# Attention: VectorE's other work queued behind the last minimum, and the causal mask added to the kept row F

## The chip, the cores and the metric

The kernel runs on one core of one Trainium2 chip. A core has a matrix engine (TensorE, PE in the profile; its weight loads are shown apart as PEld), VectorE (DVE), ScalarE (ACT), GpSimd (POOL) and SyncE (SP), which issues most DMAs. Each engine takes its instructions in the order of its own queue and waits for others by semaphores. On-chip memory is SBUF, 128 partitions wide, and PSUM, into which PE adds its products. The metric is the device time of one execution, in microseconds (us).

## What is computed

One decoder layer over 1024 tokens of 1024 channels: a normed input, one combined projection, a state-space branch and an attention branch of 16 heads with 64 channels, then gated projections of both and an output projection. The change lies in the attention:

```python
scale = ATT_HEAD_DIM ** -0.5
fcum = jnp.cumsum(log_f, axis=-1)
for blk in range(seqlen // ATT_BLOCK):
    q0, q1 = blk * ATT_BLOCK, (blk + 1) * ATT_BLOCK
    s = jnp.einsum('bhqd,bhkd->bhqk', q[:, :, q0:q1], k[:, :, :q1]).astype(jnp.float32) * scale
    s = s + fcum[:, :, q0:q1, None] - fcum[:, :, None, :q1]
    qpos = q0 + jnp.arange(ATT_BLOCK)
    kpos = jnp.arange(q1)
    s = jnp.where(kpos[None, :] <= qpos[:, None], s, -jnp.inf)
    prob = jax.nn.softmax(s, axis=-1)
    outs.append(jnp.einsum('bhqk,bhkd->bhqd', prob.astype(v.dtype), v[:, :, :q1]))
```

`fcum` at the query's own place falls out of the softmax, so only the row F = `fcum` over the keys is needed. The mask concerns one 128x128 square in each block of 128 queries: the one on the diagonal.

## The kernel before

**Two kinds of work are woven together.** All projections are a `Stream` of steps. One step is 12 matmuls of 128x512 into one PSUM bank (`pb`, `pc` or `pd`); `half()` issues half of one. The weights of a step come from DMA into a `raw` tile, or are sums of two or more of them (`total`, L357, and L373, L381). `split` then makes the tile `wop` of two parts: ScalarE rounds the weights (L351) and VectorE subtracts that from the weights (L352). `prepare` does this three steps ahead of the step that is being started, and `load_more` then loads the next `raw` tiles. The other operand of later steps is split too, by `ops.some()` (L278, L281). A finished bank goes out by `keep` (L404, ScalarE) or `give` (L414 to L418, VectorE). Gate products (L1062), stores from GpSimd's queue (L195, L1063, L1533) and a chain of subtractions on GpSimd (L213, in `differences`) come with the steps as small chores.

**The attention loop** goes over eight head pairs (two heads e = 0, 1 in each, in the lower and the upper 64 partitions). A pair has six visits, one for each of `GROUPS` (L1317): a pair of query blocks and a half h of the 1024 keys. In order these are blocks (7,6) with the upper half, (7,6) lower, (5,4) upper, (5,4) lower, (3,2) lower, (1,0) lower. A visit, in the order in which the program issues it:

1. `scores` for both blocks u = 0, 1. For each: six matmuls into two tiles `s`, one for each head. If the block has its diagonal in this half, four more matmuls of a bfloat16 pair (`eye`, `far`) add 1e30 at the keys that lie ahead of the query. Then for each head VectorE adds F to the scores and takes the minimum of the row in one instruction (L1467; F is the tile `fb`, keys sign-flipped so that the minimum is the softmax's shift), and ScalarE takes the exponential with its sum (L1471).
2. `weighted`: the products of the visit before with V, into `av`; after a second half of keys, `free` (L1419) takes `av` out.
3. What was held over (`release`), the small statistics (`settle`, `scale`), and the stream's halves "ahead".
4. `loads` for later visits, and `turned`: the exponentials are transposed on PE into `pt` (L133), and copied out as `p` by ScalarE (L1502) or VectorE (L1500).
5. `out` (L1425, L1431, L1432), then the halves "behind". In these, `ops.some()` is put into a list (`hold`) and done at the next visit's `release`.

So PE's queue reads scores, products, stream, transposes, stream, scores.

**What sets the order.** A scheduler orders each engine's queue by its own estimate of when an instruction is ready. Three tools bind it: `mm`, `turn` and `pin` keep an instruction behind everything written before it on its engine, so PE's order is as written; `tc.high_priority()` puts a block ahead of other ready work; `tc.issue_after(x)` queues everything in a block that is on x's engine behind x. The minima and exponentials are pinned and of high priority. VectorE work that is not pinned may be placed between them, or ahead of the first.

**Tiles that matter.** `fb` holds F for one half of keys and both heads, copied to all partitions, and is one tile for each half; it is loaded in `load_k`, once for a head pair. `small()` gives one of four tiles (tag `th`) that evicted gate values, fetched blocks, `st` and `rb` share. `wop` has four tiles, `raw` six, the scores' and transposes' banks `s` four.

Of the kernel before, what the change touches and what calls it, by code (L numbers as in the profile page):

```python
# [8 lines left out]
F32 = mybir.dt.float32  # L9
# [7 lines left out]
P = 128  # L17
# [69 lines left out]
def hybrid_layer(ctx: ExitStack, tc, a, out):  # L87
# [368 lines left out]
    class Stream:  # L456
# [6 lines left out]
        def __init__(self, pairs, double, last):  # L463
            self.pairs = pairs
            for n, p in enumerate(pairs):
                p.bank, p.other = (pj, "be"[n % 2]), (pjx, "d") if n < double else (pj, "c")

                p.between = n < double or n >= last

            p, q, r = pairs[0:3]  # L470
            self.steps = [(p, 1), (q, 1), (p, 2), (q, 2)] + [(p, n) for n in (6, 5, 7, 4, 3)]
            self.steps += [(q, 6), (q, 5), (q, 7), (r, 1), (q, 4), (q, 3)]
            for n in range(2, last):
                p, nxt = pairs[n], pairs[n + 1]
# [12 lines left out]
            self.building = []  # L487
            self.chores, self.line = [], []
            self.held = None
            self.count = 0  # L490
# [39 lines left out]
        def half(self):  # L530
            if self.run is None:
                if self.at == len(self.steps):
                    return False
                p, which = self.steps[self.at]
                if which == 7 and p.ops is ops_a and "merged" not in fin:
                    return False
                if p.ops is ops_a and not all(p.ops.ready(OPERAND[which].strip("-"), j) for j in range(KH)):
                    return False
                self.ahead(False)
                for ops in self.building:  # L540
                    ops.some(OPERAND[which])
                self.run = p.do(which)
                next(self.run)
            else:
                for _ in self.run:
                    pass
                self.run = None
                p, which = self.steps[self.at]
                if p in self.following:
                    ops = self.following[p]  # L550
                    if ops not in self.building:
                        self.building.append(ops)
                    ops.open(OPERAND[which])
                self.ahead(True)
                self.at += 1
            for ops in self.building:
                if self.held is None:
                    ops.some()
                else:
                    self.held.append(ops)  # L560
# [16 lines left out]

        def release(self):
            held, self.held = self.held or [], None
            for ops in held:  # L580
                ops.some()

        def do_chores(self):
            while self.chores:
# [710 lines left out]
    with tc.tile_pool(name="att", bufs=1, reuse_waits="tile", side="right") as ap, tc.tile_pool(  # L1295
# [1 line left out]
    ) as pp:  # L1297
        rows = [slice(64 * e, 64 * e + 64) for e in range(2)]

        eye = ap.tile([P, 192], BF16, name="eye")  # L1300
        far = ap.tile([P, 192], BF16, name="far")
        nc.vector.memset(eye, 0.0)
        big, beyond = small("big"), small("beyond")
        nc.vector.memset(big[:, 0:192], -NEG)
        for e in range(2):
            nc.vector.tensor_copy(eye[rows[e], 64:P], ident[rows[e], rows[e]])
            nc.gpsimd.affine_select(
                beyond[:, 192 * e : 192 * e + 192], big[:, 0:192], [[1, 192]], ALU.is_gt, 0.0, base=64 * e - 64,
                channel_multiplier=-1,
            )  # L1310
            nc.vector.tensor_copy(far[rows[e], :], beyond[rows[e], 192 * e : 192 * e + 192])

        corner = [(eye[:, 64:192], far[:, 64:192]), (eye[:, 0:P], far[:, 0:P])]

# [123 lines left out]
        def scores(hp, g, u):  # L1438
# [8 lines left out]
            diagonal = h == i // 4  # L1447
            for m, (x, y) in enumerate(ops):
                for e in range(2):
                    mm(  # L1450
                        s[e][:, 0:w], x[rows[e]], y[rows[e]], start=(m == 0), stop=(m == 2 and not diagonal),
                        skip_group_check=True,
                    )
            if diagonal:
                for n, (x, y) in enumerate(corner):
                    for e in range(2):
                        mm(
                            s[e][:, w - P : w], x[rows[e]], y[rows[e]], start=False, stop=(n == 1),
                            skip_group_check=True,
                        )  # L1460
            hd = heads[hp]
            for e in range(2):
                o = ex[:, e, u, 0:w]
                nm = hd.at(hd.nm, i, h, e)
                with tc.high_priority():
                    pin(
                        nc.vector.tensor_tensor_reduce(  # L1467
                            o, s[e][:, 0:w], fb[hp, h][:, e, 0:w], 1.0, 3.0e38, ALU.add, ALU.min, nm
                        )
                    )  # L1470
                    pin(nc.scalar.activation(o, o, AF.Exp, scale=-1.0, bias=nm, accum_out=hd.at(hd.sm, i, h, e)))  # L1471

        def turned(hp, g, sent):

# [157 lines left out]
        for m in range(6 * NK + 1):  # L1632
# [6 lines left out]
                    scores(hp, g, u)  # L1639
            for one in made:  # L1640
                weighted(*one)
            for hd, which in end(m - 1):
                hd.free(which)
            if m == 6 * NK:
                stream.release()
                heads[NK - 1].out(2)
                break
# [87 lines left out]
```

## Time and profile before

| | |
|---|---|
| timed runs | 1293.11, 1295.9 and 4353.94 us; median 1295.9 |
| profiled execution | 1292.21 us, its span 1290.5 us |
| mean granted clock of PE | 0.997 |
| attention loop, first scores to the last pair's end | 685.9 to 1127.7 us |
| minima (L1467) | 192, of 512, 384, 256 and 128 keys |
| mask matmuls | 256, in 32 of the 48 visits |

A profile shows one execution. Rows of its views read: line, engine, operation, output tile `<-` input tiles, shape, count, then busy microseconds and the mean nanoseconds of one. In a view in order of time each row begins with its start and its length in microseconds, and a bracket at the end tells how long the engine had been idle and who released it. In a view of waits a row names the waiting instruction, what ended the wait, and total, times and longest in microseconds. In a view by stretches each engine has its busy time; the last three columns are PE's granted clock, the share of the DMA engines and GB/s.

### The profile page before, as it was taken

The page shows a single profiled execution, that of the slowest core. Times are in us where ns is not written, and L with a number is a line of the kernel's source. Part 1 is how long each engine was busy: PE and PEld are TensorE (multiplying, and loading weights), DVE is VectorE, ACT ScalarE, POOL GpSimd, SP SyncE. Part 2 cuts the span into 40 slices and gives each one's busy share as a digit, 9 for nine tenths or more (in the row PEclk, how much of TensorE's full clock was granted, in tenths as well). Part 3 has the DMA queues.
Part 4 walks back from the last instruction along what each step waited for, and adds up shares of the span by engine and source line. Part 5 has one row for each costly group of instructions (what it writes and reads, how often), then busy time and mean ns, then how long its engine had stood idle before and what let it go on. Part 6 is the DMA issues. An engine that isn't in the chain of part 4 may idle for free.

```text
span 1290.5 us, 20996 instructions
## 1 busy us (share of the span) xinstructions
PE 1254.5 (97%) x7054; PEld 984.4 (76%) x7054; DVE 1006.0 (78%) x1994; ACT 796.5 (62%) x1738; POOL 259.5 (20%) x250
## 2 busy tenths in 40 slices
PE   5999999999999999999999999999999999899997
PEld 3688888887888888888877777777777776578886
DVE  7988886987788878897777567666898768776975
ACT  7745665566665665666546656666886567743754
POOL 4000440013300330124001121220001102146052
PEclk9999999999999999999999999999999999999999
DMA  8232542645336633654365665667877667656932
GB/s 297 69 115 76 161 146 91 199 143 183 128 119 204 176 130 105 212 172 115 132 211 197 203 217 198 199 221 228 256 268 238 198 213 257 205 188 194 362 113 99
DMA packets 153515, 233.57 MB, mean 181 GB/s; under 512 B 15968, under 2 KB 61504, under 8 KB 153408
## 3 DMA queue, kind: packets, MB, share of 16 engines
q1 hardware_dynamic: 137408, 197.14, 48.0%
q10 hardware_dynamic: 11136, 19.11, 3.9%
q0 software_dynamic: 4864, 15.99, 3.2%
q8 instruction: 55, 0.90, 0.3%
q14 instruction: 52, 0.43, 0.1%
HBM read 162.99 MB, written 72.34 MB: 182 GB/s over the span
## 4 chain that ended last, share of the span: by engine, by line
PE 75%; DVE 9%; DMA 7%; ACT 5%; issue 3%; SPq 1%; POOL 0%; DVEq 0%; ACTq 0%; POOLq 0%
PE pb L130 31%; PE pc L130 18%; PE pd L130 6%; PE pt L133 5%; PE av L130 4%; PE s L130 4%; PE yps L130 2%; DVE wop L352 2%; ACT ex L1471 1%; DMA xt<-in_x 1%; PE st L130 1%; DMA raw<-in_wu 1%; DVE ex L1467 1%; DVE sum L357 1%; ACT wop L351 1%
## 5 line engine op out<-in xcount | busy, mean ns | idle before, releaser
L351 ACT ACTIVATE wop<-sum 128x512 fp32r<-128x512 f32 x180 | 112.5, 626 | 113.4 <-DVE sum L357 53.8
L352 DVE TENSOR_TENSOR wop<-sum,wop 128x512 fp32r<-128x512 f32 x180 | 136.2, 758 | 54.2 <-ACT wop L351 53.3
L1471 ACT ACTIVATE ex<-ex,nm 128x512 f32<-128x512 f32 (+1 forms) x192 | 116.2, 606 | 66.1 <-DVE nm L1467 64.8
L404 ACT ACTIVATE s<-pb 128x512 f32<-128x512 f32 x144 | 85.2, 591 | 103.3 <-PE pb L130 102.7
L130 PE MATMUL pc<-x3h,wop 128*128 128x512 f32 x384 | 131.1, 398 | 1.5 <-DVE th L414 1.1
L130 PE MATMUL pb<-x0h,wop 128*128 128x512 f32 x384 | 131.1, 399 | 0.0
L130 PE MATMUL pc<-x2h,wop 128*128 128x512 f32 x384 | 130.8, 398 | 0.1
L130 PE MATMUL pb<-x6h,wop 128*128 128x512 f32 x384 | 129.5, 395 | 1.3 <-ACT s L404 1.3
L130 PE MATMUL pb<-x5h,wop 128*128 128x512 f32 x384 | 129.9, 396 | 0.8 <-ACT s L404 0.7
L130 PE MATMUL pb<-x4h,wop 128*128 128x512 f32 x384 | 129.0, 395 | 0.0
L352 DVE TENSOR_TENSOR wop<-raw,wop 128x512 fp32r<-128x512 f32 x144 | 102.5, 713 | 32.6 <-ACT wop L351 32.3
L1467 DVE CUSTOM_DVE_ANT_0 ex<-s,fb 128x512 f32<-128x512 f32 (+1 forms) x192 | 97.3, 552 | 20.0 <-PE s L130 20.0
L351 ACT ACTIVATE wop<-raw 128x512 fp32r<-128x512 f32 x144 | 89.7, 624 | 22.7 <-PE pc L130 15.2
L130 PE MATMUL pd<-x1h,wop 128*128 128x512 f32 x288 | 96.3, 394 | 0.0
L130 PEld LDWEIGHTS pc<-x3h,wop 128*128 128x128 f32 x384 | 72.5, 189 | 18.9 <-issue 1.6
L130 PEld LDWEIGHTS pb<-x5h,wop 128*128 128x128 f32 x384 | 72.1, 188 | 18.5 <-ACT s L404 2.1
L130 PEld LDWEIGHTS pb<-x6h,wop 128*128 128x128 f32 x384 | 72.1, 188 | 18.4 <-issue 1.7
L130 PEld LDWEIGHTS pb<-x0h,wop 128*128 128x128 f32 x384 | 72.7, 189 | 17.4 <-issue 2.7
L130 PEld LDWEIGHTS pc<-x2h,wop 128*128 128x128 f32 x384 | 72.1, 188 | 18.0 <-issue 2.8
L130 PEld LDWEIGHTS pb<-x4h,wop 128*128 128x128 f32 x384 | 72.1, 188 | 17.0 <-issue 2.2
L133 PE MATMUL pt<-ident,ex 128*128 128x128 f32 x576 | 74.3, 274 | 5.1 <-ACT ex L1471 4.5
L133 PEld LDWEIGHTS pt<-ident,ex 128*128 128x128 f32 x576 | 65.0, 140 | 15.4 <-ACT ex L1471 9.2
(310 smaller groups left out, 2917.8 us busy)
## 6 DMA issues: line engine op xcount, KB each, us to landing
raw<-in_wu SPq DMA_DIRECT2D x128, 256.0 KB
csb<-cs_dram SPq DMA_DIRECT2D x32, 256.0 KB
fb<-f_dram SPq DMA_DIRECT2D x16, 512.0 KB
rb<-st_dram SPq DMA_DIRECT2D x48, 128.0 KB
wd<-in_wo SPq DMA_DIRECT2D x40, 128.0 KB
xt<-in_x SPq DMA_DIRECT2D x8, 512.0 KB
gs_dram<-th ACTq DMA_DIRECT2D x16, 256.0 KB
qh_dram<-th ACTq DMA_DIRECT2D x16, 256.0 KB
```

Of the source, the lines that this page charges most:

```text
L130: return tc.keep_in_program_order(nc.tensor.matmul(*args, **kw))
L133: return tc.keep_in_program_order(nc.tensor.transpose(out_, in_, idn))
L351: nc.scalar.activation(op[:, 0], src, AF.Copy)
L352: nc.vector.tensor_tensor(op[:, 1], src, op[:, 0], ALU.subtract)
L357: self.adds.tensor_tensor(t, x, y, ALU.add)
L404: nc.scalar.activation(s, ps, AF.Copy)
L1467: nc.vector.tensor_tensor_reduce(o, s[e][:, 0:w], fb[hp, h][:, e, 0:w], 1.0, 3.0e38, ALU.add, ALU.min, nm)
L1471: pin(nc.scalar.activation(o, o, AF.Exp, scale=-1.0, bias=nm, accum_out=hd.at(hd.sm, i, h, e)))
```

## The change

Three things. **The mask:** the matmuls of `eye` and `far` go. A tile `beyond` (128x128, float32) holds 1e30 where a key lies ahead of the query and 0 elsewhere, and a new function `corner(hp, i, engine)` adds it in place to the 128 columns of F that belong to block i, for both heads. A minimum that must see these columns unmasked comes earlier in the loop's order, one that must see them masked comes later. For the first block of a visit GpSimd adds, issued in `loads` of the visit before (blocks 5, 3 and 1, and block 7 of the next pair); for the second block VectorE adds, between the minima of the first block and those of the second.

**The order:** `scores` notes its last minimum as `stream.front`. `prepare`, `ops.some()`, `free` and the deferred subtractions (`first`, `second`, `last` in `outputs`) run inside `stream.behind()`, so that their VectorE instructions are queued behind that minimum.

**The hold:** in the halves "behind", `prepare` too is put into the list, and done at the next visit's `release`, with its `load_more`.

```diff
         def prepare(self, p, which):
-            p.prepare(which)
+            if self.held is not None:
+                self.held.append(lambda: self.prepare(p, which))
+                return
+            with self.behind():
+                p.prepare(which)
             self.load_more()
+
+        def behind(self):
+
+            return nullcontext() if self.front is None else tc.issue_after(self.front)
...
         def release(self):
             held, self.held = self.held or [], None
-            for ops in held:
-                ops.some()
+            for fn in held:
+                with self.behind():
+                    fn()
...
-        eye = ap.tile([P, 192], BF16, name="eye")
-        far = ap.tile([P, 192], BF16, name="far")
...
-        corner = [(eye[:, 64:192], far[:, 64:192]), (eye[:, 0:P], far[:, 0:P])]
+        beyond = ap.tile([P, P], F32, name="beyond")
+        big = small("big")
+        nc.vector.memset(big[:, 0:P], -NEG)
+        nc.gpsimd.affine_select(beyond, big[:, 0:P], [[1, P]], ALU.is_gt, 0.0, base=0, channel_multiplier=-1)
...
+        def corner(hp, i, engine):
+
+            f = fb[hp, i // 4][:, :, i % 4 * P : i % 4 * P + P]
+            pin(engine.tensor_tensor(f, f, beyond.unsqueeze(1).to_broadcast([P, 2, P]), ALU.add))
...
-            if diagonal:
-                for n, (x, y) in enumerate(corner):
-                    for e in range(2):
-                        mm(
-                            s[e][:, w - P : w], x[rows[e]], y[rows[e]], start=False, stop=(n == 1),
-                            skip_group_check=True,
-                        )
             hd = heads[hp]
+            if u and h == i // 4:
+                with tc.high_priority():
+                    corner(hp, i, nc.vector)
             for e in range(2):
                 o = ex[:, e, u, 0:w]
                 nm = hd.at(hd.nm, i, h, e)
                 with tc.high_priority():
-                    pin(
+                    least = pin(
                         nc.vector.tensor_tensor_reduce(
                             o, s[e][:, 0:w], fb[hp, h][:, e, 0:w], 1.0, 3.0e38, ALU.add, ALU.min, nm
                         )
                     )
                     pin(nc.scalar.activation(o, o, AF.Exp, scale=-1.0, bias=nm, accum_out=hd.at(hd.sm, i, h, e)))
+            stream.front = least.ins
...
             hp, g = divmod(m, 6)
             more = hp + 1 < NK
+            if g in (1, 3, 4):
+                corner(hp, {1: 5, 3: 3, 4: 1}[g], nc.gpsimd)
+            if g == 4 and more:
+                corner(hp + 1, 7, nc.gpsimd)
...
         for _ in range(14):
             stream.half()
+        corner(0, 7, nc.gpsimd)
...
-            for hd, which in end(m - 1):
-                hd.free(which)
+            with stream.behind():
+                for hd, which in end(m - 1):
+                    hd.free(which)
...
-            for fn in deferred:
-                fn()
+            with stream.behind():
+                for fn in deferred:
+                    fn()
```

More of the change, by code (lines that the diff above doesn't have):

```diff
@@ L489, in __init__ @@
             self.held = None
+            self.front = None
             self.count = 0
@@ L557, in half @@
                 if self.held is None:
-                    ops.some()
+                    with self.behind():
+                        ops.some()
                 else:
-                    self.held.append(ops)
+                    self.held.append(ops.some)
             for chores in (self.chores, self.line):
@@ L579, in release @@
             held, self.held = self.held or [], None
-            for ops in held:
-                ops.some()
+            for fn in held:
+                with self.behind():
+                    fn()
         def do_chores(self):
@@ L1298, in hybrid_layer @@
         rows = [slice(64 * e, 64 * e + 64) for e in range(2)]
-        eye = ap.tile([P, 192], BF16, name="eye")
-        far = ap.tile([P, 192], BF16, name="far")
-        nc.vector.memset(eye, 0.0)
-        big, beyond = small("big"), small("beyond")
-        nc.vector.memset(big[:, 0:192], -NEG)
-        for e in range(2):
[L1306 to L1309, printed above, removed]
-            )
-            nc.vector.tensor_copy(far[rows[e], :], beyond[rows[e], 192 * e : 192 * e + 192])
-        corner = [(eye[:, 64:192], far[:, 64:192]), (eye[:, 0:P], far[:, 0:P])]
+        beyond = ap.tile([P, P], F32, name="beyond")
+        big = small("big")
+        nc.vector.memset(big[:, 0:P], -NEG)
+        nc.gpsimd.affine_select(beyond, big[:, 0:P], [[1, P]], ALU.is_gt, 0.0, base=0, channel_multiplier=-1)
         GROUPS = [((7, 6), 1), ((7, 6), 0), ((5, 4), 1), ((5, 4), 0), ((3, 2), 0), ((1, 0), 0)]
@@ L1446, in scores @@
             ops = [(t[:, x, isl], keys[:, y, 0:w]) for x, y in ((0, 0), (0, 1), (1, 0))]
-            diagonal = h == i // 4
             for m, (x, y) in enumerate(ops):
@@ L1450, in scores @@
                     mm(
-                        s[e][:, 0:w], x[rows[e]], y[rows[e]], start=(m == 0), stop=(m == 2 and not diagonal),
-                        skip_group_check=True,
-                    )
-            if diagonal:
-                for n, (x, y) in enumerate(corner):
-                    for e in range(2):
-                        mm(
-                            s[e][:, w - P : w], x[rows[e]], y[rows[e]], start=False, stop=(n == 1),
-                            skip_group_check=True,
-                        )
+                        s[e][:, 0:w], x[rows[e]], y[rows[e]], start=(m == 0), stop=(m == 2), skip_group_check=True,
+                    )
             hd = heads[hp]
+            if u and h == i // 4:
+                with tc.high_priority():
+                    corner(hp, i, nc.vector)
             for e in range(2):
@@ L1646, in hybrid_layer @@
                 heads[NK - 1].out(2)
+                stream.front = None
                 break
```

## The prediction

> **What bounds the kernel now.** I read the page first, then the stretches of the attention stage, then one visit of it on each engine, then the waits.
>
> ```profile
> PE 1254.5 (97%) x7054; PEld 984.4 (76%) x7054; DVE 1006.0 (78%) x1994; ACT 796.5 (62%) x1738; POOL 259.5 (20%) x250
> ...
> PE 75%; DVE 9%; DMA 7%; ACT 5%; issue 3%; SPq 1%; POOL 0%; DVEq 0%; ACTq 0%; POOLq 0%
> ```
>
> TensorE (PE) is busy 97% of the span and carries 75% of the chain that ended last. The change touches only the attention loop, so I cut that loop into its eight head pairs of six visits (the matmuls `s<-k,q` mark the visits). These are the fifth pair, the eighth, and the sum over all eight; the columns are busy microseconds in that stretch.
>
> ```profile
> 915.90:966.90 51.00, 50.35 (x356) 37.24 (x355) 46.20 (x122) 43.79 (x107) 2.16 (x4) 1.00 0.84 282
> ...
> 1071.20:1127.70 56.50, 51.14 (x350) 36.24 (x349) 44.87 (x109) 40.20 (x101) 11.13 (x14) 1.00 0.74 246
> sum 441.80, PE 434.94 PEld 326.15 DVE 319.87 ACT 296.74 POOL 59.36; mean PE 54.37 PEld 40.77 DVE 39.98 ACT 37.09 POOL 7.42
> ```
>
> PE is idle for 441.8 − 434.9 = 6.9 us of the loop, 5.4 of them in the last pair. VectorE (DVE) is busy 72% (319.9 of 441.8) but 91% in the fifth pair (46.2 of 51.0); GpSimd (POOL) is busy 13%. So two things can shorten the loop: fewer PE instructions, and the 6.9 us. Nothing else on PE changes, and PE's order is written out by the program.
>
> **The change: the matmuls that go.** Two visits on PE, the first with a diagonal block in each half, the second without one, and then a short diagonal visit:
>
> ```profile
> 800.82 0.99 PE L130 MATMUL s<-k,q 64*128 64x512 f32 x6
> 801.62 0.28 PE L130 MATMUL s<-far,eye 64*128 64x128 bf16 x3
> 801.72 0.42 PE L130 MATMUL s<-k,q 64*128 64x384 f32 x1
> ...
> 802.33 0.32 PE L130 MATMUL s<-far,eye 64*128 64x128 bf16 x4
> 802.58 0.87 PE L130 MATMUL av<-p,v 128*64 128x256 f32 x8
> ...
> 811.02 1.66 PE L130 MATMUL s<-k,q 64*128 64x512 f32 x12
> 812.61 1.62 PE L130 MATMUL av<-p,v 128*64 128x256 f32 x14
> ```
>
> ```profile
> 822.21 0.29 PE L130 MATMUL s<-far,eye 64*128 64x128 bf16 x4
> 822.30 0.53 PE L130 MATMUL s<-k,q 64*128 64x128 f32 x6
> 822.67 0.29 PE L130 MATMUL s<-far,eye 64*128 64x128 bf16 x4
> 822.89 1.30 PE L130 MATMUL av<-p,v 128*64 128x256 f32 x10
> ```
>
> ```profile
> L130 PE MATMUL s<-far,eye 64*128 64x128 bf16 x256 | 18.9, 221 | 0.0
> ```
>
> Matmuls overlap, so I count from start to start. From the first mask matmul to the next other one: 0.10 + 0.25 = 0.35 us in the first visit, 0.09 + 0.22 = 0.31 in the short one. A cross-check: the visit without a diagonal takes 1.59 us for 1024 columns of scores, so 896 columns cost 1.39, and the first visit took 1.76, which is 0.37 more. There are 256 / 8 = 32 such visits: 32 x 0.33 = 10.6 us. The ends are 0 (PE waits elsewhere instead) and 18.9, the group's busy time, in which overlap with neighbours counts twice. I take 10.6, since starts are what moves the next instruction.
>
> **The order of VectorE.** In the first visit of the last pair:
>
> ```profile
> 1072.74 0.29 PE L130 MATMUL s<-far,eye 64*128 64x128 bf16 x4
> ```
>
> ```profile
> 1075.78 0.68 DVE L281 TENSOR_TENSOR x0l<-x0l,x0h 128x512 fp32r<-128x512 f32 x1
> 1076.38 0.68 DVE L1467 CUSTOM_DVE_ANT_0 ex<-s,fb 128x512 f32<-128x512 f32 x1
> ...
> 1077.60 0.68 DVE L281 TENSOR_TENSOR x0l<-x0l,x0h 128x512 fp32r<-128x512 f32 x1
> 1078.20 0.55 DVE L1467 CUSTOM_DVE_ANT_0 ex<-s,fb 128x384 f32<-128x384 f32 x1
> ```
>
> ```profile
> 1077.16 0.72 ACT L1471 ACTIVATE ex<-ex,nm 128x512 f32<-128x512 f32 x1 [4.15 <-DVE nm L1467]
> ```
>
> ```profile
> PEld pt L133 <- ACT ex L1471: 9.2, 18, 1.1
> ```
>
> ```profile
> 1129.81 0.27 PE L133 MATMUL tp<-ident,ns 128*8 128x128 f32 x1 [2.13 <-DVE ns L1376]
> ```
>
> The scores lay ready from about 1073.0 and the first minimum (L1467) came at 1076.38, with another split (L281) between the minima. ScalarE then waited 4.15 us, and behind it the transposes (L133). The change puts splits, weight sums and the products of `free` behind the last minimum, and holds the weight work of a visit's later halves over to the next visit. What it can give back is those 6.9 us and the 2.13 us just behind the loop, 9.0 together; `o<-o,rb`, evictions and gate products are not queued, so part of the delay stays. I take 3.5, the ends are 0 and 9.0.
>
> What is late next is the held work, above all the weight halves:
>
> ```profile
> 835.81 0.68 DVE L352 TENSOR_TENSOR wop<-sum,wop 128x512 fp32r<-128x512 f32 x1
> ```
>
> ```profile
> 849.24 0.39 PE L130 MATMUL pc<-x3h,wop 128*128 128x512 f32 x1
> ```
>
> I paired the 78 weight halves of the loop (L352) in order with the steps that use them. Of those made inside the loop, this one has the shortest time from ready to used: 849.24 − 836.49 = 12.75 us. A hold lasts less than one visit, 51.0 / 6 = 8.5 to 56.5 / 6 = 9.4 us. So I cost it at nothing; without that cover each late half would cost PE up to its 0.68 us. On SyncE's queue the weight loads follow the held sums, by the same part of a visit; their tiles are read several steps later, so again nothing, with one 0.68 us stall for each late tile as the other end.
>
> **The adds on VectorE.** 32 adds over 128x256, ahead of the second block's minima.
>
> ```profile
> L1432 DVE TENSOR_TENSOR zr<-o 128x256 f32<-128x256 f32 x16 | 6.8, 423 | 0.3
> ```
>
> 32 x 0.42 = 13.4 us of VectorE. Beside it runs ScalarE: one exponential takes 0.72 us against 0.68 for a minimum, so after two exponentials the third minimum has some slack, and the scores come 0.1 us earlier. On the path I count 0; uncovered it is 0.42 in each of the 18 waits of the transposes, 7.6 us.
>
> **The adds on GpSimd.** 32 of them, each half the size of the subtraction here, so 0.65 us:
>
> ```profile
> 801.87 1.29 POOL L213 TENSOR_TENSOR x<-x,th 128x512 f32<-128x512 f32 x1
> ```
>
> ```profile
> 802.07 1.65 DVE L352 TENSOR_TENSOR wop<-raw,wop 128x512 fp32r<-128x512 f32 x1 [1.06 <-ACT wop L351]
> ```
>
> ```profile
> 715.50 1.28 POOL L213 TENSOR_TENSOR th<-x,th 128x512 f32<-128x512 f32 x1 [17.20 <-DMA th<-ys_dram]
> ```
>
> ```profile
> 716.11 0.69 DVE L1467 CUSTOM_DVE_ANT_0 ex<-s,fb 128x512 f32<-128x512 f32 x1
> ...
> 717.33 0.69 DVE L1467 CUSTOM_DVE_ANT_0 ex<-s,fb 128x512 f32<-128x512 f32 x1
> ```
>
> While GpSimd subtracted, a VectorE subtraction took 1.65 us in place of 0.68; a minimum beside it took its usual 0.69. Hence each of the 32 adds may hold a VectorE instruction by up to 0.65 us, 20.8 us of VectorE in all, but it falls right behind the last minimum, where the queued work is not urgent. Only the fifth pair lacks room: 46.2 + 4 x 0.42 + 4 x 0.65 = 50.5 us of work in 51.0 − 1.3 = 49.7. I count +1, with ends 0 and 20.8. [...]
>
> The adds that follow groups 3 and 4 wait for the last minimum, and what is behind them on GpSimd waits too. The subtraction at 715.50 would start after 718.02 + 0.65 = 718.7, so 3.2 us later, and with it its small tile comes free, one of four that the evictions of PE's banks share. I count +2 for that, from 0 to 3.2 in each of some four such places, 13.
>
> The sum, against the profiled execution (1292.2 us, 1.7 over its span): 1292.2 − 10.6 − 3.5 + 1 + 2 = 1281.1. The two timed runs near it, 1293.1 and 1295.9 (also the median of the three), lie 2.3 above the profiled one in the mean; so I forecast 1281.1 + 2.3 = 1283.
>
> **Rivals.** *The path moves to the minima.* With two halves of PE work or fewer in a visit of the later pairs, PE has less to do between scores and transposes; there the 10.6 would only lengthen the wait. For it: the 18 waits above; against: in the seven pairs before the last PE idles 6.9 − 5.4 = 1.5 us together. Half the gain stays: 1292.2 − 5.3 + 2 = about 1289, 1291 in a timed run.
>
> *GpSimd's holds land on the path.* All 20.8 in place of 1: 1281.1 + 19.8 = 1300.9, timed 1303. It decides where VectorE's work after a minimum is urgent, as an eviction of a PE bank is. Against it: at 802.07 the held subtraction delayed PE nowhere that the waits show. [...]
>
> *Slower: a mask add stuck in GpSimd's queue.* The next visit's first minimum waits for it.
>
> ```profile
> POOL ya_dram L1533 <- DVE zr L1432: 74.2, 6, 30.1
> ...
> POOL ya_dram L1533 <- DVE zr L1425: 57.3, 5, 16.9
> ```
>
> ```profile
> 946.24 0.69 DVE L1467 CUSTOM_DVE_ANT_0 ex<-s,fb 128x512 f32<-128x512 f32 x1
> ...
> 952.54 0.68 DVE L1467 CUSTOM_DVE_ANT_0 ex<-s,fb 128x512 f32<-128x512 f32 x1
> ```
>
> From a last minimum (ending 946.93) to the next first one there are 5.6 us in the tight fifth pair. It decides once a store ahead of the add waits longer than that after the minimum: the 11 waits, less 5.6 each, are 131.5 − 61.6 = 69.9 us; were half of it on the path, 1281.1 + 35.0 = 1316, and all of it 1351; the middle is 1334, timed 1336. Against it: these waits began with GpSimd idle, and the stores belong to an earlier visit (801.32, just as the next one's scores began).
>
> *Much faster.* The group's whole 18.9 and all 9.0: 1292.2 − 27.9 = 1264, timed 1267.
>
> **How the numbers follow.** Forecast 0.58 (1273 to 1290); path moved 0.12; holds 0.15; stuck add 0.11; much faster 0.04. Within 2% (about what a measurement of this kernel can tell from no change; 1270 to 1321) lie the first three: 0.85; faster 0.04, slower 0.11. The low end, 1273, lies just under the sum with the full 9.0 and without the 3 us of new costs (1292.2 − 10.6 − 9.0 = 1272.6, timed 1275); the high end, 1304, takes in the holds. Left out are the stuck add, the much faster case and the tails, some 0.17.
>
> **What would show it.** No `s<-far,eye` rows; diagonal visits about 0.33 us shorter on PE; no split, sum or weight row between minima but the mask add of about 0.42; PE's idle time in the loop under 6.9; PE's row of waits on the minima empty. I am wrong if minima wait for GpSimd, if matmuls `pb` or `pc` wait for weight halves or evictions, or if the transposes wait more than 9.2 us for the exponentials.

## The result, and the profile after

| | before | changed |
|---|---|---|
| median of 18 runs | 1294.09 us | 1291.15 us |
| ratio, first set | | 0.9981 [0.9971, 0.9991] |
| median, second set | 1293.25 us | 1289.84 us |
| ratio, second set | | 0.9972 [0.9959, 0.9984] |
| profiled execution, span | 1292.21, 1290.5 us | 1290.98, 1289.3 us |

The change gains 2.5 to 3.6 us, where 11.1 were forecast against the profiled execution. That it lies within 2% was right, the size was not. In the first execution of the changed kernel (4334.7 us) PE was busy for 4310.5 us with its 6798 matmuls, against the 1249.3 below; it and the 4353.94 of the kernel before are left out, and the profile below is of the second set.

The busy time of each engine in the changed kernel:

```profile
PE 1249.3 (97%) x6798; PEld 982.4 (76%) x6798; DVE 1025.1 (80%) x2021; ACT 798.8 (62%) x1738; POOL 292.7 (23%) x281
```

The 256 instructions are gone, but PE is busy only 5.2 us less (1254.5 to 1249.3). The short diagonal visit of the third pair, in order of time on PE, shows where they were:

```profile
820.26 0.90 PE L130 MATMUL s<-k,q 64*128 64x256 f32 x12
821.09 1.95 PE L130 MATMUL av<-p,v 128*64 128x256 f32 x16
```

The scores take 0.83 us from start to start, where before 1.14 passed (821.75 to 822.89 there): 0.31 less. So did nearly every steady visit (one that waits for nothing) with a diagonal: in the first four pairs the third, fifth and sixth visit went from 8.14, 10.96 and 7.81 us to 7.81, 10.67 and 7.50.

The loop by stretches, one for each pair; the fifth and the eighth, and the sum (busy us of PE, PEld, DVE, ACT, POOL, with instructions; then granted clock, DMA share, GB/s):

```profile
912.10:966.40 54.30, 51.55 (x326) 37.50 (x325) 48.70 (x124) 43.97 (x107) 6.29 (x8) 0.97 0.79 268
...
1067.60:1131.10 63.50, 54.14 (x318) 38.65 (x317) 50.64 (x119) 41.44 (x104) 14.82 (x17) 0.92 0.66 218
sum 445.00, PE 430.92 PEld 324.40 DVE 339.95 ACT 299.63 POOL 89.92; mean PE 53.87 PEld 40.55 DVE 42.49 ACT 37.45 POOL 11.24
```

From first scores to the end of the last pair's transposes the loop took 443.9 us before and 445.0 now: no gain at all in this execution. The lengths of the pairs, counted from scores to scores (the last one to the transposes behind it), tell where:

| pair | 1 | 2 | 3 | 4 | 5 | 6 | 7 | 8 |
|---|---|---|---|---|---|---|---|---|
| before | 57.2 | 57.7 | 57.7 | 57.4 | 51.0 | 49.7 | 54.6 | 58.6 |
| changed | 57.8 | 56.1 | 56.1 | 56.1 | 54.2 | 47.9 | 53.4 | 63.5 |

Five pairs gain 1.3 to 1.8 us each, 7.6 together. The first, fifth and eighth lose 8.7. The clock column shows one part of that loss: in pairs 5 and 8 PE was granted 0.97 and 0.92 of its clock. These are the stretches themselves, in the changed kernel:

```profile
933.80:937.20 3.40, 3.40 (x17) 1.73 (x14) 3.40 (x13) 3.40 (x13) 0.00 (x0) 0.51 0.66 228
1094.20:1097.60 3.40, 3.36 (x10) 2.61 (x11) 3.27 (x9) 1.90 (x7) 0.00 (x0) 0.50 0.40 132
1121.50:1128.30 6.80, 6.80 (x32) 4.63 (x33) 3.20 (x12) 3.41 (x11) 0.54 (x1) 0.50 0.35 120
```

and the only such stretch near the loop in the kernel before, just behind its end:

```profile
1130.20:1133.60 3.40, 3.40 (x14) 2.02 (x12) 2.15 (x4) 2.49 (x6) 0.00 (x0) 0.50 0.09 31
```

At half the clock I count half of these 13.6 us as lost, 6.8 us: an estimate from the clock column. With it the loop adds up to within a microsecond: −10.6 for the matmuls, as forecast, +5.1 for idle PE (9.0 us before, counted to the same end, 14.1 now), +6.8 for the clock: +1.3, where +1.0 was measured. What follows the loop gained 2.5 us (160.7 to 158.2), 1.7 of them the stretch that lay there before. The timed runs show the loss of clock too, but a smaller one: in the second set the mean clock is 0.9943 over the 12 executions of the changed kernel and 0.9966 over the 23 of the kernel before. The difference, 0.0023 of 1290 us, is about 3 us by the same estimate.

PE's waits in the changed loop (waiting instruction, what ended the wait; total us, times, longest), with VectorE's wait for scores on top:

```profile
DVE ex L1467 <- PE s L130: 37.9, 26, 3.2
...
PEld s L130 <- ACT p L1503: 10.2, 11, 3.9
...
PE s L130 <- ACT p L1503: 6.6, 5, 3.5
PEld pt L133 <- ACT ex L1471: 6.6, 13, 1.5
...
PE pt L133 <- DVE nm L1467: 1.9, 1, 1.9
```

And the two rows of the kernel before to compare with:

```profile
DVE ex L1467 <- PE s L130: 20.0, 16, 2.6
...
PEld s L130 <- ACT p L1502: 3.3, 7, 1.2
```

The minima do come sooner: VectorE now waits for scores more than before (37.9 against 20.0 us), and the transposes' loads wait 6.6 us for exponentials instead of 9.2. But the next scores wait for the copies `p` of the transposes: 10.2 us on the loads, where it was 3.3 before, and 6.6 on the matmuls, where it was 1.2. The wait moved from one side of the transposes to the other.

### The profile page after: what moved, and what is told of

It is laid out like the page before. It is cut to its first block, busy times and chain, and to the rows that moved or that the text cites. A ratio compares the mean times of both kernels' runs of the same rounds, so it can differ in the third digit from the quotient of the medians.

```text
span 4333.0 us, 20609 instructions
## 1 busy us (share of the span) xinstructions
PE 4310.5 (99%) x6798; PEld 2214.8 (51%) x6798; DVE 1025.2 (24%) x2021; ACT 826.2 (19%) x1738; POOL 266.2 (6%) x281
## 4 chain that ended last, share of the span: by engine, by line
PE 99%; DVE 0%; ACT 0%; DMA 0%; issue 0%; DVEq 0%; SPq 0%; ACTq 0%
PE pb L130 44%; PE pc L130 25%; PE pd L130 8%; PE pt L133 6%; PE av L130 5%; PE s L130 4%; PE yps L130 2%; PE st L130 1%; PE tr L133 1%; PE tr L130 1%; PE tr_v L133 1%; PE df L130 0%; PE pv L130 0%; PE pt_f L130 0%; PE pt_cs L130 0%; PE pv_t L133 0%
## 5 line engine op out<-in xcount | busy, mean ns | idle before, releaser
L130 PE MATMUL pc<-x3h,wop 128*128 128x512 f32 x384 | 386.9, 1104 | 0.0
L130 PE MATMUL pb<-x6h,wop 128*128 128x512 f32 x384 | 385.6, 1099 | 0.7 <-ACT s L404 0.7
L130 PE MATMUL pb<-x0h,wop 128*128 128x512 f32 x384 | 385.7, 1099 | 0.0
L130 PE MATMUL pb<-x5h,wop 128*128 128x512 f32 x384 | 383.2, 1096 | 0.7 <-ACT s L404 0.7
L130 PE MATMUL pc<-x2h,wop 128*128 128x512 f32 x384 | 383.1, 1096 | 0.0
L130 PE MATMUL pb<-x4h,wop 128*128 128x512 f32 x384 | 382.7, 1093 | 0.0
L130 PE MATMUL av<-p,v 128*64 128x256 f32 (+1 forms) x640 | 239.8, 993 | 0.0
L130 PE MATMUL pb<-x6l,wop 128*128 128x512 f32 x192 | 210.9, 1098 | 0.0
L130 PE MATMUL pb<-x5l,wop 128*128 128x512 f32 x192 | 210.9, 1098 | 0.0
L130 PE MATMUL pb<-x0l,wop 128*128 128x512 f32 x192 | 210.6, 1097 | 0.0
```

The lines of the kernel that those rows point to most:

```text
L130: return tc.keep_in_program_order(nc.tensor.matmul(*args, **kw))
```

## The experiments

Two questions: does the ordering, or do the adds, eat the gain; and can either be dropped? My theory was that the matmuls are worth what was forecast and that the losses come with the rest; the rivals were that the matmuls were never on the path, and that the queueing helps as forecast while the adds cost much more. Effects below are (ratio − 1) x 1293 us, with the interval worked out likewise.

**The matmuls alone.** The kernel before, with the mask left out:

```diff
-                        s[e][:, 0:w], x[rows[e]], y[rows[e]], start=(m == 0), stop=(m == 2 and not diagonal),
+                        s[e][:, 0:w], x[rows[e]], y[rows[e]], start=(m == 0), stop=(m == 2),
...
-            if diagonal:
+            if False:
```

> The kernel before without its 256 mask matmuls; the causal mask is left out altogether, the rest of the computation is as before. It prices the matmuls alone. The prediction's term: 10.6 us under before. Theory A: under 5 us. Theory C: the mean granted clock falls, as in the changed kernel, and a part of the 10.6 us is missing.

Measured 1285.16 us, 0.9941 [0.9926, 0.9957]: −7.6 us [−9.6, −5.6]. In its profile the loop fell from 443.9 to 434.7, 9.2 us, though PE idled 0.5 more. 9.2 + 0.5 = 9.7 us of PE's instructions, so the 10.6 was nearly right as work, and the timed runs got 7.6 of it. Their mean clock was 0.9955, against 0.9966 in the kernel before; that is 1.4 us of the rest, by the estimate from the clock. (The half-clock stretch that begins in the last 2.2 us of this loop cost little there: PE was busy for 0.10 us of them.)

**The order alone.** Queueing and hold as in the change, the mask by matmuls as before:

```diff
+        def behind(self):
+            return nullcontext() if self.front is None else tc.issue_after(self.front)
...
+            with self.behind():
+                p.prepare(which)
...
             if diagonal:
                 for n, (x, y) in enumerate(corner):
```

> The order and the hold as in the change, the mask still by matmuls as before. If the order costs time: 5 to 10 us over before. If it does what the prediction said: 2 to 9 us under before. If it matters to nothing: within 1 us of before.

Measured 1293.07 us, 1.0000 [0.9988, 1.0013]: 0.0 us [−1.6, +1.7]. Nothing is gained. Its fifth pair takes 54.9 us (51.0 before), so that loss needs no add. The first visit of its last pair, at which the prediction had looked, does fall from 11.5 to 8.5 us.

**The mask alone.** The adds as in the change, but no queueing and no hold:

```diff
         def prepare(self, p, which):
-            if self.held is not None:
-                self.held.append(lambda: self.prepare(p, which))
-                return
-            with self.behind():
-                p.prepare(which)
+            p.prepare(which)
             self.load_more()
...
         def behind(self):
...
-            return nullcontext() if self.front is None else tc.issue_after(self.front)
+            return nullcontext()
```

> The mask added to F as in the change, but nothing queued behind the minimum and nothing held over. If the new order costs time (B, by the order), this gains what the matmuls gave, 8 to 12 us under before. If the adds on VectorE and GpSimd cost it (B, by the adds), or the matmuls were worth little (A), 0 to 4 us under before.

Measured 1305.62 us, 1.0095 [1.0076, 1.0114]: +12.3 us [+9.8, +14.7]. Against the kernel with no mask at all, the 64 adds cost 1305.6 − 1285.2 = 20.4 us. The first visit of its second pair, in order of time, shows how:

```profile
745.58 0.68 DVE L1463 CUSTOM_DVE_ANT_0 ex<-s,fb 128x512 f32<-128x512 f32 x1
...
746.19 1.03 DVE L373 TENSOR_TENSOR sum<-sum,raw 128x512 f32<-128x512 f32 x1
...
747.14 0.68 DVE L1421 TENSOR_TENSOR o<-av,zr 128x512 f32<-128x512 f32 x1
...
747.74 0.41 DVE L1337 TENSOR_TENSOR fb<-fb,beyond 128x256 f32<-128x256 f32 x1
...
748.19 0.56 DVE L1463 CUSTOM_DVE_ANT_0 ex<-s,fb 128x384 f32<-128x384 f32 x1
...
749.78 0.33 PE L133 MATMUL pt<-ident,ex 128*128 128x128 f32 x1 [1.25 <-ACT ex L1467]
...
750.79 0.44 PE L133 MATMUL pt<-ident,ex 128*128 128x128 f32 x2 [0.69 <-ACT ex L1467]
```

The add sits between the second and the third minimum, and a sum and a product have slipped in ahead of it. So the third minimum starts 1.9 us after the second one ended, where the add alone takes 0.41, and the transposes wait 1.25 us, then 0.69 more. Counted over the loop, 60 VectorE instructions of over 0.3 us, besides the adds, stand between the minima of a visit here, 28 in the kernel before and 2 in the changed one. Over the loop the loads of the transposes wait for exponentials (9.2 us in the kernel before):

```profile
PEld pt L133 <- ACT ex L1467: 27.0, 33, 2.7
```

**Which of the adds.** As in the kernel just shown, without queueing and hold, and only VectorE's 32 adds; the half of the mask that GpSimd adds is left out:

```diff
-            if g in (1, 3, 4):
-                corner(hp, {1: 5, 3: 3, 4: 1}[g], nc.gpsimd)
-            if g == 4 and more:
-                corner(hp + 1, 7, nc.gpsimd)
...
-        corner(0, 7, nc.gpsimd)
```

> The mask adds without the new order, and of these only VectorE's 32 between the minima; the blocks that GpSimd would mask (7, 5, 3, 1) stay unmasked, so half of the mask is left out. The mask adds without the order cost 20 us over the kernel without a mask (1305.6 against 1285.2). If VectorE's adds between the minima make it, since other work slips in with them: 1300 or more. If GpSimd's adds make it (its queue, or its hold on VectorE): 1285 to 1290.

Measured 1306.58 us, 1.0111 [1.0091, 1.0130]. VectorE's adds make all of it; GpSimd's add nothing that can be seen.

**The order without adds.** The changed kernel without any add; the mask is left out:

```diff
-            if u and h == i // 4:
-                with tc.high_priority():
-                    corner(hp, i, nc.vector)
```

and the calls on GpSimd as above.

> The changed kernel without any mask add, so the causal mask is left out; the order and the hold stay. It prices the 64 adds under the new order. If the adds cost what the changed kernel lost (Q): 8 to 11 us under before, like the kernel without mask matmuls. If the order costs it (L): 3 to 5 us under before, and the fifth pair stays near 54 us against 51.0.

Measured 1285.53 us, 0.9954 [0.9940, 0.9968]: −5.9 us [−7.8, −4.1]. Against no mask and no order (−7.6) the order seems to cost 1.7 us, though the intervals overlap; it gains nothing here either. Against the change itself (−2.5 and −3.6) the adds cost 2.3 to 3.4 us under the order, not 20.

The fourth visit of its last pair lasts 14.5 us where before it took 10.5. The minima are on time, but on ScalarE two splits stand ahead of the exponentials, and the first of them waits 4.10 us for its load; so the transposes wait. Then ScalarE has a split, an eviction, a weight split and four more splits ahead of the first copy, while PE runs at half clock (1097.2 to 1104.0):

```profile
1098.29 0.61 ACT L280 ACTIVATE x1h<-x1l 128x512 fp32r<-128x512 f32 x1
...
1099.29 0.61 ACT L351 ACTIVATE wop<-sum 128x512 fp32r<-128x512 f32 x1
1099.80 1.13 ACT L280 ACTIVATE x5h<-x5l 128x512 fp32r<-128x512 f32 x2
1100.84 1.13 ACT L280 ACTIVATE x3h<-x3l 128x512 fp32r<-128x512 f32 x2
1101.88 0.57 ACT L1500 ACTIVATE p<-pt 128x512 f32<-128x512 f32 x1
```

**The hold.** The changed kernel, `prepare` no longer held over:

```diff
         def prepare(self, p, which):
-            if self.held is not None:
-                self.held.append(lambda: self.prepare(p, which))
-                return
             with self.behind():
```

> The changed kernel, but the weight work of a visit's later halves is not held over; the queueing behind the minimum stays. If the hold makes the lump (L): the fifth pair falls from 54.2 us to about 51, and the kernel is 2 to 4 us faster than the changed one. If the queueing alone makes it: the fifth pair stays at 54. If the hold is what keeps sums and splits from between the minima: 5 us or more slower, towards the kernel with the mask adds alone (1305.6).

Measured 1289.06 us, 0.9982 [0.9966, 0.9997]: the change without its hold is as fast as with it (0.9972, 0.9981). The place of the loss moved: pairs 1, 5 and 8 take 60.0, 51.6 and 58.9 us. So the loss of the fifth pair comes from the hold: the queueing is still there, and the pair is back near the 51.0 of before. In the four kernels with the order and the hold in every pair it takes 53.4 to 54.9 us.

**All adds on VectorE.**

```diff
-                corner(hp, {1: 5, 3: 3, 4: 1}[g], nc.gpsimd)
+                corner(hp, {1: 5, 3: 3, 4: 1}[g], nc.vector)
...
-                corner(hp + 1, 7, nc.gpsimd)
+                corner(hp + 1, 7, nc.vector)
...
-        corner(0, 7, nc.gpsimd)
+        corner(0, 7, nc.vector)
```

> The changed kernel with all 64 mask adds on VectorE, none on GpSimd. Theory Q (an add stuck in GpSimd's queue, and GpSimd holding VectorE): the third visit of the last pair falls from 11.2 us towards 6.8, the fifth from 13.7 towards 10.5, and the kernel gains 3 to 7 us over the changed one. Theory L (VectorE's queue itself, a lump of queued work ahead of an eviction): 32 more adds of 0.42 us make the fifth and the last pair longer, and the kernel is 0 to 5 us slower than the changed one.

Measured 1291.82 us, 0.9996 [0.9983, 1.0009]. Taking GpSimd out of it gains nothing: pairs 1, 5 and 8 take 60.2, 54.4 and 63.0 us. In the last pair the third visit falls from 11.2 to 6.5 us, but the fifth stays at 13.9 (13.7 in the changed kernel). GpSimd's queue is therefore not the main cause.

**The changed kernel again**, unedited:

> The changed kernel once more, for a profile at PE's full rate. Theory A (the mask's matmuls were worth less than 10.6 us on PE): visits with a diagonal are shorter by clearly less than 0.33 us each and PE's idle time in the loop is about as before, 7 us. Theory B (new waits give it back): those visits are shorter by 0.33 us, and PE's idle time, in the loop or behind it, is 8 to 10 us more than before. Theory C (the granted clock gives it back): PE's matmuls start to start take about 0.5% longer, at a mean granted clock of 0.992 to 0.995 against 0.997. Time 2.5 us under the kernel before.

Measured 1289.84 us, 0.9972 [0.9959, 0.9984]; its profile is the one shown above.

**The change where it pays.** If pairs 2 to 4, 6 and 7 gain and the others lose, the others should keep matmuls. First the fifth and the last pair, with narrower mask matmuls (64 columns, or 64 keys). In these kernels `beyond` is a bfloat16 tile, a second difference, not priced apart.

```diff
+        marks = [(eye[:, 64:P], far, 0), (eye, far[:, 0:64], 64)]
+        added = {0, 1, 2, 3, 5, 6}
...
         def corner(hp, i, engine):
+            if hp not in added:
+                return
...
-            stream.front = least.ins
+            stream.front = least.ins if hp in added else None
```

and `prepare` is held only while `front` is set.

> The change in six head pairs; in the fifth and the last the mask is by matmuls (over 64 columns of queries or keys in place of 128, to fit) and nothing is queued or held. If the loss sits in these two pairs, as the visits say: the fifth near 51, the last near 58.6, the others as in the changed kernel, the loop 437 us against 444.0, and the kernel 6 to 8 us under before. If it is spread, or moves on to the next pair: 2 to 4 us under before.

Measured 1289.67 us, 0.9972 [0.9957, 0.9987], the same as the change, though its profiled loop took 437.8 us.

Then the first pair as well:

```diff
-        added = {0, 1, 2, 3, 5, 6}
+        added = {1, 2, 3, 5, 6}
```

> As the hybrid, and the first head pair too has its mask by matmuls, with nothing queued or held. If the adds cost only in visits where VectorE or ScalarE is late already: the first visit of the loop falls from 11.1 us to about 9.7, the loop is about 436 us, and the kernel is 6 to 8 us under before, 1 to 2 under the hybrid. If the spread from run to run hides it: no difference from the hybrid (0.997).

Measured 1286.26 us, 0.9949 [0.9934, 0.9963]: by the medians some 3 us under the change. About half of its distance from the kernel with six pairs is clock, by the same estimate: the mean over the timed runs is 0.9967 here and 0.9955 there, 1.5 us. Then also no queueing in the last visit ahead of a pair that keeps its matmuls:

```diff
-            stream.front = least.ins if hp in added else None
+            stream.front = least.ins if hp in added and (g < 5 or hp + 1 in added) else None
```

> As the kernel with five pairs, but in the last visit before a pair without adds nothing is queued or held either. If what was held in that visit makes the fifth pair longer (52.9 us in the hybrid against 51.0): it falls to 51.0 to 51.5, and the kernel gains 1 to 2 us on the one with five pairs. Otherwise the same within 0.5 us.

Measured 1287.74 us, 0.9958 [0.9944, 0.9972], no different from the one before it. In the first pair, the narrow matmuls took, in the third visit:

```profile
705.01 0.62 PE L130 MATMUL s<-k,q 64*128 64x256 f32 x6
705.56 0.38 PE L130 MATMUL s<-far,eye 64*64 64x128 bf16 x4
...
706.55 1.95 PE L130 MATMUL av<-p,v 128*64 128x256 f32 x16
```

1.54 us from start to start, 0.40 more than the wide ones (1.14) that have more columns. So the last kernel has in the three pairs one matmul for each head over all 128 rows, in place of two over 64:

```diff
-                for n, (x, y, c) in enumerate(marks):
-                    for e in range(2):
...
+                for e in range(2):
+                    mm(s[e][:, w - P : w], eye, beyond, start=False, stop=True, skip_group_check=True)
```

> As the kernel with five pairs, but in the other three pairs the mask is one matmul of 128 rows for each head in place of two narrow ones of 64 rows. In the kernel with five pairs the narrow mask matmuls (64 columns of queries, or 64 keys) made the diagonal visits 0.4 us longer than the wide ones of the kernel before (8.53 against 8.15, 11.35 against 10.96, 8.22 against 7.81). If that is a price of their narrow form: these visits fall to 8.15, 10.96 and 7.81 or below, the loop to about 437 us, and the kernel to 8 to 11 us under before. If it is a price of any switch between weights of 64 rows and other shapes: they stay at 8.5, 11.3 and 8.2, and the kernel at 0.995 of before.

Measured 1285.27 us, 0.9934 [0.9915, 0.9953]: −8.5 us [−11.0, −6.1], the fastest kernel here that applies the whole mask, and its interval lies apart from that of the change, though not from those of the two kernels before it. The matmuls themselves are hardly cheaper: 709.00 to 710.47 = 1.47 us in the same visit.

```profile
709.00 0.62 PE L130 MATMUL s<-k,q 64*128 64x256 f32 x6
709.55 0.29 PE L130 MATMUL s<-beyond,eye 128*128 128x128 bf16 x2
...
710.47 1.95 PE L130 MATMUL av<-p,v 128*64 128x256 f32 x16
```

## Why the prediction was right or wrong

**The matmuls, −10.6: right as PE's work, 3.0 us too large as time.** Steady visits are shorter by 0.29 to 0.34 us each, as worked out from start to start, and 0.33 had been said. Timed alone the matmuls are worth 7.6 [5.6, 9.6]. That "starts are what moves the next instruction" holds in the visits where PE waits for nothing; in the rest some of the time comes back as waiting and as lost clock.

**The order of VectorE, −3.5: the step that failed.** It held that VectorE's lateness ahead of the minima was what PE waited for, and it costed the moved work at nothing, because the held weight halves had 12.75 us of room. Measured, order alone gives 0.0, and with the matmuls gone about +1.7. The gain that it looked for was there: with the order alone ScalarE waits 0.88 us for the first minimum of the last pair, where it had waited 4.15, and that visit is 3.0 us shorter. But the time came back elsewhere: 3.9 us in the fifth pair, 2.0 and 0.9 in the fourth and the fifth visit of the last. What failed is the zero for the moved and held work. It changes the order in which ScalarE does its own work, and then the copies `p` come late. In the fifth pair of the changed kernel:

```profile
924.90 0.69 DVE L352 TENSOR_TENSOR wop<-sum,wop 128x512 fp32r<-128x512 f32 x1
...
925.50 1.29 DVE L278 SCALAR_TENSOR_TENSOR x4l<-x4l,x4h 128x512 fp32r<-128x512 f32 x2
...
926.71 0.68 DVE L357 TENSOR_TENSOR sum<-raw 128x512 f32<-128x512 f32 x1
...
927.38 0.68 DVE L416 TENSOR_TENSOR th<-pc,s 128x512 f32<-128x512 f32 x1
...
928.10 0.63 ACT L632 ACTIVATE th<-th 128x512 f32<-128x512 f32 x1 [1.98 <-DVE th L416]
...
930.73 1.66 ACT L280 ACTIVATE x1h<-x1l 128x512 fp32r<-128x512 f32 x3
...
932.29 0.59 ACT L1503 ACTIVATE p<-pt 128x512 f32<-128x512 f32 x1
...
932.93 0.55 PE L130 MATMUL s<-k,q 64*128 64x128 f32 x5 [1.38 <-ACT p L1503]
```

and in the kernel before, at the same place:

```profile
930.98 1.13 ACT L280 ACTIVATE x1h<-x1l 128x512 fp32r<-128x512 f32 x2
932.02 0.62 ACT L621 ACTIVATE th<-th 128x512 f32<-128x512 f32 x1
...
935.22 0.55 PE L130 MATMUL s<-k,q 64*128 64x128 f32 x5 [0.28 <-ACT p L1502]
```

Read the first downward. Behind the last minimum, which ends at 925.0, the queued work follows in one lump, then comes the eviction L416. It is not later than it was: it starts 2.4 us after the end of that minimum, 2.3 us in the kernel before. What changed is ScalarE's order. The tanh of that eviction is now its next instruction behind the exponentials, so ScalarE idles 1.98 us. Before, it had two splits `x4h`, a weight split and two of the four splits `x1h` to do ahead of that tanh, and did not idle. Now all four `x1h` fall between copies, and PE waits 1.38 us for the last copy, where it waited 0.28. Less than a microsecond later the half-clock stretch of 933.8 begins. The kernel with the order alone shows the same chain, tanh wait of 1.98 included, and there PE waits 1.68 us.

The kernel without the hold tells which part does it. The queueing is still there and the eviction again starts 2.3 us after the minimum, but ScalarE has its old order, PE waits 0.45 us at that place, and the pair takes 51.6 us. So in this pair it is the hold. Why the scheduler then puts the tanh ahead is not shown. The prediction looked for the next late thing among the held weight halves. These were hardly ever late (one wait of 0.4 us), but the copies were. Apart from that wait, none of its three signs of being wrong came; the wait of the next scores for copies was not among them.

**The hold, 0: right in sum, by luck.** It could have been left out: without it the ratio is 0.9982. But by the profiles it costs 2.6 us in the fifth pair (54.2 against 51.6) and 4.6 in the eighth, and gives 2.2 in the first.

**VectorE's adds, 0, and GpSimd's, +3: together right in sum, for a reason that was not given.** Under the order all 64 cost 2.3 to 3.4 us, though one on GpSimd took 0.73 us (at 1091.37) and another 1.13 (at 1112.16, both below) where 0.65 had been counted. The forecast took VectorE's adds as free beside ScalarE, which is nearly so only because nothing else may stand between the minima. Without that, the 64 cost 20.4. This is the use of the ordering here: it doesn't gain, it keeps the adds from costing. One place where they do cost is the loop's first visit, 11.3 us in the changed kernel and 9.7 with the order and no adds: the later minima come later, on ScalarE an eviction and a weight split get ahead of the last exponential, and the transposes wait 0.64 and 1.27 us.

Two long visits of the last pair look like what had been priced as a bound or as a rival. GpSimd's hold, in the fifth:

```profile
1112.16 1.13 POOL L1341 TENSOR_TENSOR fb<-fb,beyond 128x256 f32<-128x256 f32 x1 [7.32 <-DVE nm L1467]
...
1112.60 2.94 DVE L281 TENSOR_TENSOR x5l<-x5l,x5h 128x512 fp32r<-128x512 f32 x2
...
1113.24 1.74 POOL L373 TENSOR_TENSOR sum<-sum,raw 128x512 f32<-128x512 f32 x1
...
1116.65 1.28 DVE L281 TENSOR_TENSOR x3l<-x3l,x3h 128x512 fp32r<-128x512 f32 x2
...
1120.37 0.27 ACT L1399 ACTIVATE st<-pt 8x128 f32<-8x128 f32 x1 [1.22 <-DVE th L1073]
...
1120.96 1.26 PE L130 MATMUL s<-k,q 64*128 64x256 f32 x5 [3.51 <-ACT p L1503]
```

The pair of subtractions takes 2.94 us beside GpSimd's add and sum, 1.28 when alone (at 1116.65). VectorE is then late with a gate product; `st` needs a small tile that this product frees; the copies stand behind `st`; PE waits 3.51 us and then runs 6.8 us at half clock. But the add on GpSimd is not what makes this visit long. With all adds on VectorE the visit takes 13.9 us, with a wait of 3.63 us. With the order and no adds it takes 10.5.

The slower rival, a mask add stuck in GpSimd's queue, came near once, in the third:

```profile
1086.76 0.90 PE L130 MATMUL s<-k,q 64*128 64x256 f32 x12
...
1087.80 0.69 DVE L1431 TENSOR_TENSOR zr<-o,rb 128x512 f32<-128x512 f32 x1 [4.10 <-DMA rb<-st_dram]
...
1089.25 1.60 POOL L357 TENSOR_TENSOR sum<-sum,raw 128x512 f32<-128x512 f32 x1 [9.73 <-DVE wop L352]
1089.61 3.05 DVE L278 SCALAR_TENSOR_TENSOR x4l<-x4l,x4h 128x512 fp32r<-128x512 f32 x2
...
1091.37 0.73 POOL L1341 TENSOR_TENSOR fb<-fb,beyond 128x256 f32<-128x256 f32 x1
...
1092.59 0.41 DVE L1467 CUSTOM_DVE_ANT_0 ex<-s,fb 128x256 f32<-128x256 f32 x1
...
1093.06 0.27 PE L133 MATMUL pt<-ident,ns 128*8 128x128 f32 x1 [1.93 <-DVE nm L1467]
```

Its scores were ready by 1087.7, the add ended at 1092.1, and the minimum came at 1092.59, as the splits ahead of it on VectorE ended. The add was late, but it was not the last thing that the minimum waited for. Both hang on one load of `rb` that VectorE waited 4.10 us for. This visit takes 11.2 us instead of 6.8; with all adds on VectorE, and with none, it takes 6.5. But then another visit of that pair is long, so this place is one among several.

**The rival "the path moves to the minima" fell**, as the waits above show: PE waited for a minimum once, 1.9 us, and the path moved to the copies. The time that it gave, about 1291 us in a timed run, is what was measured; that is luck.

**What was in no term:** the half clock. It took 6.8 us of the loop in the profiled execution, and by the mean clocks about 3 us more than before in the timed runs, both as estimated above.

**The sum by runs:** −7.6 for the matmuls, +1.7 for the order, +2.3 to +3.4 for the adds, against −10.6, −3.5 and +3 in the forecast. That these make the measured −3.6 to −2.5 is no proof: each term is the difference of two neighbouring kernels, so they must. What they show is where the forecast's 8 us went: 5.2 in the order, 3.0 in the matmuls, nothing in the adds. Each is good to some 2 or 3 us, so the 1.7 in particular is not apart from nothing. How much pairs 1, 5 and 8 lose differs from kernel to kernel; I followed the places shown here and not all of them. Why narrowing the change to six pairs gave no gain, and to five pairs did, stays open.

## What to carry to other kernels

Work taken from the bounding engine is worth its start-to-start time only in the stages where what feeds that engine keeps up (here five pairs gained 7.6 us and three lost 8.7): compare stage by stage, and keep the old form in those that lose. Moving low-priority work on one engine, and holding it over above all, also changes the order of work on the engines that feed it or use it; look at their queues for the next late thing, and not only at the work that was moved. A step added inside a chain of urgent instructions must be bound so that nothing slips in beside it. Here 64 adds cost 20.4 us without that, and 2.3 to 3.4 with it.

## What the runs showed of the hardware

**Half clock followed some short waits of PE.** After waits of 1.38, 1.93 and 3.51 us (rows above) the granted clock was 0.50 for 3.4, 3.4 and 6.8 us, by the estimate from the clock worth another 1.7, 1.7 and 3.4. Before, 2.13 us at the loop's end was followed by one such stretch. Over the timed runs the mean clock was 0.9918 with the mask alone and 0.9966 in the kernel before. The length of the wait alone does not decide it. Waits of 0.64 and 1.27 us in the loop's first visit passed without in the changed kernel: a matmul of 512 columns just behind took 0.39 us (at 694.82), and the clock of that pair was 1.00. With the mask alone, waits of 1.25 and 0.69 us (rows above) were followed by the same kind of matmul at 0.63 us (at 752.54), and 0.39 again at 755.03. What decides it is not shown.

**Fewer columns cost more here.** The narrower mask matmuls, and the single one over 128 rows, took 0.40 and 0.33 us more in a visit than the pair over 64 rows (1.54 and 1.47 against 1.14 us), though they have fewer columns. The pair has the tile shape of the scores around it, 64\*128; half of the narrow ones have 64\*64, and the single one has 128\*128. Whether it is the change of shape between neighbours that costs is not shown by itself.
